# Writing the tokens' scales to DRAM as ten rows of 512 bytes, after a transpose on TensorE

## The chip, the core and the metric

The kernel runs on one core of one Trainium2 chip. The metric is the device time of one execution, in microseconds (us). Engines are named as in the profile: PE is TensorE (PEld its weight loads), DVE is VectorE, ACT is ScalarE, POOL is GpSimd, and SP is the engine that issues most of the transfers.

## What is computed

One encoder layer over 1280 tokens (1024 of a prompt, 256 of a sample) of width 1024, in float32. Only the beginning matters here:

```python
def _rms_norm(x, g, eps):
    xf = x.astype(jnp.float32)
    y = xf * lax.rsqrt(jnp.mean(xf * xf, axis=-1, keepdims=True) + eps)
    return (y * g.astype(jnp.float32)).astype(x.dtype)
...
    n = _rms_norm(h, g_mix, NORM_EPS)
    z = jnp.einsum('bsd,dc->bsc', n, w_in).astype(f32)
    cuts = np.cumsum([A_Q_COLS, A_K_COLS, A_V_COLS, B_Q_COLS, B_K_COLS]).tolist()
    qa, ka, va, qb, kb, vb = jnp.split(z, cuts, axis=-1)
```

Two attention mixers (A: four differential heads; B: eight query heads on two key heads), an output projection, an MLP of width 4096, a gated embedding and a last norm follow. All of that is the same before and after.

## The kernel before

The projection multiplies the tokens, scaled by `g_mix` but not yet by the norm, with blocks of `w_in`; the norm's factor, one number per token, is applied to the result. Each float32 operand is split into a high and a low part, and three matmuls are done for each product: high by high, high by low, low by high.

The factors are in `rstd1`, a tile of 128 partitions by 10 columns: token `128 t + p` stands at partition `p`, column `t`. Where tokens lie on partitions (units for B's q and k, and for v: `b_unit`, `va_unit`), a column of `rstd1` is used directly. Where tokens lie along the free dimension (`qk_unit`, for A's q and k), the factors are needed as a row that is the same on all 128 partitions: the tile `R`, 128 x 1280. It is made through DRAM: `rstd1` is written into the DRAM tensor `rd` in the order of tokens (L439), and `rd` is read back into `R`, broadcast to all partitions (L440). Since neighbouring elements of a row of `rstd1` are 128 tokens apart in `rd`, the write is made of 1280 single elements of 4 bytes.

The stages around it, in the order of the program:

- `b_unit(2, w_kv)`, woven with `va_unit(0, w_va0)`: B's k and v, and half of A's v, for the token tiles 0 to 9. Each token tile gives a PSUM tile `psb` (L241), which `norm_rope` turns into `ro` with many small operations on VectorE, ScalarE and POOL; TensorE transposes `ro` into `trb` two tiles later (L324).
- small constants (`gple`, `gmlp`, `gsub`, `lam_t`), then `rd` and `R`
- `b_unit(0, ...)` woven with `va_unit(1, ...)`, and then `b_unit(1, ...)` woven with `qk_a(0)`, the first that reads `R`.

Weights come in blocks. `load_w` brings 256 KB into `rawp` (a unit of 256 columns has four such blocks) or `rawa` (128 columns, two blocks), makes the high part on ScalarE (`whp` or `wha`, L176) and the low part on VectorE or POOL (`wlp` or `wla`, L177). Six buffers hold `rawp`, ten each hold `whp` and `wlp`. In what follows the twelve `rawp` of the units after the constants are counted from 1; number 6 is the second block of `va_unit(1)`.

Which instruction stands where in an engine's row is set by a scheduler that follows the program and a simulated time line; each engine then executes its row in order. Transfers issued by `dma` and `load` all stand in SP's row; loads of weights keep their order among themselves. `pp1` holds PSUM tiles, of which those of the tag "pb" (`psb`) have two buffers, used in turn.

Of the kernel before, what the change touches and what calls it, by code (L numbers as in the profile page):

```python
# [14 lines left out]
F32 = mybir.dt.float32  # L15
F32R = mybir.dt.float32r
F16 = mybir.dt.float16
AF = mybir.ActivationFunctionType
# [5 lines left out]
P = 128  # L24
# [5 lines left out]
NT = T // P  # L30
# [15 lines left out]
def encoder_kernel(ctx: ExitStack, tc: tile.TileContext, x, xT, pT, w_in, w_out, w_ff1, w_ff2, w_gate, w_proj,  # L46
# [39 lines left out]
    V, S, G, PE = nc.vector, nc.scalar, nc.gpsimd, nc.tensor  # L86
    dma = nc.sync.dma_start
# [9 lines left out]
    def pool(name, bufs=1, side=None, space=None, stack=None):  # L97
        kw = dict(name=name, bufs=bufs, reuse_waits="tile")
        if side:
            kw["side"] = side  # L100
        if space:
            kw["space"] = space
        return (stack or ctx).enter_context(tc.tile_pool(**kw))
# [14 lines left out]
    ident = cp.tile([P, P], F32, name="ident")  # L118
# [33 lines left out]
    rstd1 = cp.tile([P, NT], F32, name="rstd1")  # L152
# [55 lines left out]
    bp = pool("bp", side="left", bufs=2, stack=bs)  # L208
    ppj = pool("ppj", bufs=2, space=PSUM)
    pp1 = pool("pp1", bufs=1, space=PSUM, stack=bs)  # L210
# [224 lines left out]
    V.tensor_scalar(neglam, neglam, -LAM_INIT, None, op0=ALU.add)  # L435


    rd = dp.tile([1, T], F32, name="rd")
    dma(rd.rearrange("a (t p) -> p (a t)", p=P), rstd1)  # L439
    dma(R, rd.to_broadcast([P, T]))  # L440

    weave(b_unit(0, wload(1536, dma=load)), va_unit(1, wload(1280, dma=load)), 1.0)
# [1110 lines left out]
```

## Time and profile before

| what | value |
|---|---|
| median of 3 runs | 1733.48 us (1733.33 to 1734.53) |
| the profiled execution, time | 1731.98 us |
| the profiled execution, span from first to last instruction | 1730.2 us |
| PE busy | 1676.3 us (97% of the span) |
| DVE, ACT, POOL busy | 1180.3 us, 859.7 us, 703.0 us |
| mean granted clock of TensorE | 0.992 |
| DMA packets | 189111, of which 14512 under 512 B |

Times within the profile are counted from the start of the span. A row of a timeline gives start, length, engine, line, operation, output and inputs; what stands in brackets is how long the engine had been idle before it, and who released it. A row of the chain of waits gives start, length and what the time went to. A row of transfers gives their number, the KB of each, and the time from issue to landing.

### The profile page before, as it was taken

To read this page: it belongs to the slowest core of one execution; us is meant where nothing else is said; L and a number is where in the kernel's file an instruction comes from. 1 tells how busy PE (TensorE), PEld (TensorE's weight loads), DVE (VectorE), ACT (ScalarE), POOL (GpSimd) and SP (SyncE) were. 2 spreads that over 40 slices of the span, in tenths; PEclk is the share of its full clock that TensorE was granted. 3 is DMA by queue.
4 is the path that set the end of the run, shared out by engine and by line. 5 is a ranking of instruction groups with operands and counts; after the bars stand their busy time and mean duration, and the time that the engine had idled before them with its cause. 6 is when DMAs were issued, how large, how long until landed. Compare 5 with 4: busy or idle time off the path is not lost.

```text
span 1730.2 us, 27230 instructions
## 1 busy us (share of the span) xinstructions
PE 1676.3 (97%) x9848; PEld 1493.9 (86%) x9848; DVE 1180.3 (68%) x2104; ACT 859.7 (50%) x1730; POOL 703.0 (41%) x677
## 2 busy tenths in 40 slices
PE   8799999999899999998999999999999999999997
PEld 8799888888788888877999999998888888888886
DVE  7567578777877878578766666665764855354666
ACT  8423377776776757665323332333433333344554
POOL 1123455545564445346765656530533400001442
PEclk9999999999999999998999999999999999999999
DMA  9832573433963523382433433349676365532111
GB/s 320 218 117 100 179 189 113 128 110 93 257 187 120 157 76 108 103 257 97 140 138 130 154 124 137 128 167 388 205 233 194 123 208 190 174 113 83 39 43 49
DMA packets 189111, 263.60 MB, mean 152 GB/s; under 512 B 14512, under 2 KB 121904, under 8 KB 188976
## 3 DMA queue, kind: packets, MB, share of 16 engines
q1 hardware_dynamic: 187232, 256.60, 46.6%
q0 software_dynamic: 1600, 5.24, 1.0%
q8 instruction: 78, 1.28, 0.3%
q14 instruction: 57, 0.47, 0.1%
q10 hardware_dynamic: 144, 0.00, 0.0%
HBM read 175.29 MB, written 81.27 MB: 148 GB/s over the span
## 4 chain that ended last, share of the span: by engine, by line
PE 85%; DVE 5%; issue 3%; DMA 3%; ACT 2%; POOL 1%; SPq 0%; POOLq 0%; DVEq 0%; ACTq 0%
PE psa L241 6%; PE sc L569 6%; PE av L647 5%; PE psg L157 5%; PE pso L241 5%; PE psb L241 4%; PE tr L623 4%; PE psv L241 3%; PE psp L157 1%; DMA rawp<-in_w_in 1%; DMA h_sb<-in_w_out 1%; DVE pl L634 1%; DVE p L604 1%; PE f__16266 L157 1%; PE f__15226 L157 1%
## 5 line engine op out<-in xcount | busy, mean ns | idle before, releaser
L569 PE MATMUL sc<-kt,qt 128*128 128x512 f32 (+1 forms) x576 | 156.4, 390 | 11.3 <-ACT p L594 5.2
L1262 ACT ACTIVATE ao<-ar 128x1280 fp32r<-128x1280 f32 x56 | 71.3, 1274 | 191.1 <-PE f__16270 L157 37.9
L1264 DVE TENSOR_TENSOR ao<-ar,ao 128x1280 fp32r<-128x1280 f32 x56 | 95.4, 1705 | 98.0 <-ACT ao L1262 98.0
L634 DVE TENSOR_TENSOR pl<-tr,ph 128x512 fp32r<-128x512 f32 x204 | 137.9, 684 | 35.4 <-ACT ph L629 34.4
L629 ACT ACTIVATE ph<-tr 128x512 fp32r<-128x512 f32 x204 | 120.1, 595 | 58.2 <-PE tr L623 47.1
L241 PE MATMUL pso<-ow,mt 128*128 128x512 f32 x480 | 124.1, 402 | 4.1 <-DMA mt<-md 2.5
L569 PEld LDWEIGHTS sc<-kt,qt 128*128 128x128 f32 x576 | 98.4, 189 | 29.9 <-DVE mm L582 7.0
L1044 POOL TENSOR_SCALAR w1r<-w1r,gmlp 128x256 f32<-128x256 f32 x128 | 108.4, 863 | 38.5 <-DMA w1r<-in_w_ff 19.0
L623 PE MATMUL tr<-ident,p 128*128 128x128 f32 x768 | 115.7, 273 | 4.1 <-DVE pl L634 3.3
L157 PE MATMUL psg<-gw,n 128*128 128x512 f32 (+1 forms) x504 | 115.2, 384 | 0.0
L623 PEld LDWEIGHTS tr<-ident,p 128*128 128x128 f32 x768 | 91.6, 140 | 21.1 <-DVE pl L634 7.1
L157 PEld LDWEIGHTS psg<-gw,n 128*128 128x128 f32 x504 | 90.8, 188 | 19.5
L241 PEld LDWEIGHTS pso<-ow,mt 128*128 128x128 f32 x480 | 87.9, 191 | 21.7 <-DMA mt<-md 2.9
L647 PE MATMUL av<-ph,vt 128*128 128x256 f32 x544 | 103.0, 291 | 1.2 <-DVE o L695 0.5
L1052 ACT ACTIVATE w<-w1s 128x512 fp32r<-128x512 f32 x64 | 40.1, 628 | 125.3 <-POOL w1s L1070 6.8
L608 POOL TENSOR_SCALAR p<-p,rl 128x1024 f32<-128x1024 f32 x64 | 76.2, 1192 | 50.8 <-DVE rl L606 49.8
L586 DVE TENSOR_REDUCE mm<-sc 128x1 f32<-128x1024 f32 (+1 forms) x80 | 84.0, 1055 | 10.6 <-PE sc L569 10.0
L647 PE MATMUL av<-pl,vt 128*128 128x256 f32 x408 | 90.4, 303 | 0.2 <-DVE pl L634 0.2
L647 PEld LDWEIGHTS av<-ph,vt 128*128 128x128 f32 x544 | 82.8, 191 | 6.7 <-DVE osq L674 0.8
L594 ACT ACTIVATE p<-sc,mm 128x1024 f32<-128x1024 f32 x64 | 71.3, 1115 | 24.7 <-DVE mm L586 12.0
L1437 POOL TENSOR_TENSOR p_l<-pr,p_h 128x256 fp32r<-128x256 f32 x10 | 7.8, 782 | 182.7 <-ACT p_h L1436 182.7
L582 DVE CUSTOM_DVE_ANT_0 p<-sc,dist 128x1024 f32<-128x1024 f32 x64 | 77.5, 1217 | 5.7 <-PE tr L623 2.6
(1506 smaller groups left out, 4793.7 us busy)
## 6 DMA issues: line engine op xcount, KB each, us to landing
ar<-ad SPq DMA_DIRECT2D x56, 640.0 KB, 4.1
w2r<-in_w_ff SPq DMA_DIRECT2D x56, 512.0 KB, 4.4
qt<-qd SPq DMA_DIRECT2D x160, 128.0 KB, 3.0
ad<-q SPq DMA_DIRECT2D x64, 320.0 KB, 2.3
w1r<-in_w_ff SPq DMA_DIRECT2D x32, 512.0 KB, 3.8
ad<-qs SPq DMA_DIRECT2D x48, 320.0 KB, 2.2
md<-ml SPq DMA_DIRECT2D x40, 256.0 KB, 2.5
mt<-md SPq DMA_DIRECT2D x20, 512.0 KB, 4.8
```

The costliest lines, as they stand in the source:

```text
L157: PE.matmul(ps, a, b, start=start and i == 0, stop=stop and i == n - 1)
L241: PE.matmul(ps, a, b, start=i == 0, stop=i == n - 1)
L569: PE.matmul(ps[:, h0:h0 + n], shared["q"][:, cc, v, i * P:(i + 1) * P], kt[:, s0 + h0:s0 + h0 + n], start=v == 0, stop=v == 1)
L582: V.tensor_tensor_reduce(out=p[:, :sn], in0=ps[:, :sn], in1=dst_t[:, off:off + sn], scale=SLOPES[idx], scalar=3.0e38, op0=ALU.add, op1=ALU ...
L586: V.tensor_reduce(out=st["m", i][:, 0:1], in_=ps[:, :sn], axis=AX.X, op=ALU.max, negate=True)
L608: G.tensor_scalar(p[:, :sn], p[:, :sn], rl[:, 0:1], 1.0, op0=ALU.mult, op1=ALU.mult)
L623: PE.transpose(t[:, jj, i * P:(i + 1) * P], st["ws"][i][:, j * P:(j + 1) * P], ident)
L629: S.activation(ph, st["tr", j2], AF.Copy)
L634: V.tensor_tensor(pl, st["tr", j2], f(st["ph", j2][:]), op=ALU.subtract)
L647: PE.matmul(st["av"][:, :256], x_, y_, start=j2 == 0 and n == 0, stop=j2 == nj - 1 and n == len(pr) - 1)
L1044: G.tensor_scalar(r, r, gmlp[:, k:k + 1], 1.0, op0=ALU.mult, op1=ALU.mult)
L1264: V.tensor_tensor(ao[:, 1], a, f(ao[:, 0]), op=ALU.subtract)
```

## The change

`rstd1` is transposed on TensorE with the identity matrix into a PSUM tile of the tag "pb" (10 partitions by 128), copied to SBUF by ScalarE as `rr_t`, and written to `rd` from there: ten rows, each of 128 neighbouring tokens, 512 bytes. The read into `R` is the same.

```diff
+    rp = pp1.tile([P, 512], F32, tag="pb", name="rp", bufs=2)
+    PE.transpose(rp[:NT, :P], rstd1, ident)
+    rr_t = bp.tile([NT, P], F32, name="rr_t", bufs=1)
+    S.activation(rr_t, rp[:NT, :P], AF.Copy)
     rd = dp.tile([1, T], F32, name="rd")
-    dma(rd.rearrange("a (t p) -> p (a t)", p=P), rstd1)
+    dma(rd.rearrange("a (t p) -> (a t) p", p=P), rr_t)
     dma(R, rd.to_broadcast([P, T]))
```

Lines behind the change have numbers higher by 4: `rd`'s transfer is L439 before and L443 after, `R`'s L440 and L444.

SP's row, before, from the transfer `rd` on (`rawp` are weight blocks, here numbers 6 to 9; `vad` and `vbd` are stores of v):

```order
L439 DMA rd<-rstd_95 128x10x1
L94 DMA rawp<-in_w_in 128x2x256
L371 DMA vad_73<-vl 128x256
L371 DMA vad_74<-vl 128x256
L94 DMA rawp<-in_w_in 128x2x256 x2
L440 DMA R<-rd 128x1280
L94 DMA rawp<-in_w_in 128x2x256
```

The same place after:

```order
L94 DMA rawp<-in_w_in 128x2x256 x2
L371 DMA vad_73<-vl 128x256
L371 DMA vad_74<-vl 128x256
L94 DMA rawp<-in_w_in 128x2x256 x2
L352 DMA vbd_77<-vbl 128x128
L352 DMA vbd_78<-vbl 128x128
```

`rd` and `R` are gone from here, block 6 has moved into `rd`'s place, and 7 ahead of two stores. Both transfers now stand further on in SP's row, after the blocks of the next unit and the first `rawa`:

```order
L443 DMA rd<-rr_t 10x128
L319 DMA kd_72<-qkl 128x2x512
L94 DMA rawa<-in_w_in 128x4x128
L444 DMA R<-rd 128x1280
L94 DMA rawa<-in_w_in 128x4x128
L319 DMA kd_72<-qkl 128x2x256
```

TensorE's row at the border between the units, before (`trb` are transposes of `ro`, for tiles 7 and 8; `psb` is the first token tile of `b_unit(0)`):

```order
L241 MATMUL psv<-whp,xl 128x256
L324 MATMUL trb<-ident,ro 128x128
L241 MATMUL psb<-whp,xh 128x256
L324 MATMUL trb<-ident,ro 128x128
L241 MATMUL psb<-wlp,xh 128x256
```

And after:

```order
L241 MATMUL psv<-whp,xl 128x256
L324 MATMUL trb<-ident,ro 128x128
L439 MATMUL rp<-ident,rstd_95 10x128
L324 MATMUL trb<-ident,ro 128x128
L241 MATMUL psb<-whp,xh 128x256
```

The new transpose `rp` stands between the two others, and the first `psb` matmul behind them.

ScalarE's row a little later, before:

```order
L176 ACTIVATE whp<-rawp 128x512
L316 ACTIVATE qkl<-trb 128x512
L176 ACTIVATE wha<-rawa 128x512 x2
L284 ACTIVATE sq<-psb,rstd_95 128x256
L368 ACTIVATE vl<-psv,rstd_95 128x2x128
```

And after:

```order
L176 ACTIVATE whp<-rawp 128x512
L316 ACTIVATE qkl<-trb 128x512
L176 ACTIVATE wha<-rawa 128x512
L441 ACTIVATE rr_t<-rp 10x128
L176 ACTIVATE wha<-rawa 128x512
L284 ACTIVATE sq<-psb,rstd_95 128x256
```

The copy `rr_t` stands between the first two splits `wha` of A's weights. Further on, the rows of all engines are the same before and after but for a few neighbours that change places.

## Prediction

> **What bounds the kernel now.** I read the page first, then TensorE's waits, then the chain of waits around the change, and last the queue of SP, on which the changed transfer stands.
>
> ```profile
> PE 1676.3 (97%) x9848; PEld 1493.9 (86%) x9848; DVE 1180.3 (68%) x2104; ACT 859.7 (50%) x1730; POOL 703.0 (41%) x677
> ```
>
> TensorE is busy 97% of the span, so a change to a side transfer can only matter where TensorE stands still. The list of its waits, longest first (total, times, longest, in us), begins with the first of these rows:
>
> ```profile
> PE trb L324 <- DVE ro L302: 9.2, 2, 7.9
> ...
> PE pso L241 <- DMA mt<-md: 2.5, 1, 2.5
> ```
>
> One wait of 7.9 us is the longest of the whole kernel; the longest on a load later on, for `mt`, is 2.5. In the timeline of TensorE (start, us, engine, line) it stands here, at the border between the first projection units and the next ones:
>
> ```profile
> 65.96 0.27 PE L324 MATMUL trb<-ident,ro 128*128 128x128 f32 x1
> 65.99 0.36 PE L241 MATMUL psb<-whp,xh 128*128 128x256 f32 x1
> 74.29 0.47 PE L324 MATMUL trb<-ident,ro 128*128 128x128 f32 x1 [7.94 <-DVE ro L302]
> 74.42 0.56 PE L241 MATMUL psb<-wlp,xh 128*128 128x256 f32 x1
> ...
> 78.17 0.28 PE L241 MATMUL psv<-whp,xh 128*128 128x256 f32 x1
> 78.29 0.28 PE L241 MATMUL psv<-wlp,xh 128*128 128x256 f32 x1
> ...
> 81.83 0.28 PE L241 MATMUL psb<-whp,xh 128*128 128x256 f32 x1
> ```
>
> VectorE's `ro` is only the last link. The chain of waits tells what held it:
>
> ```profile
> 53.69 6.03 DMA rawp<-in_w_in
> ...
> 59.74 11.77 DMA rawp<-in_w_in
> ...
> 71.53 0.64 ACT whp L176
> ...
> 72.19 0.07 DVE wlp L177
> ...
> 73.31 0.25 DVE vbl L349
> ...
> 73.94 0.30 DVE ro L302
> ...
> 74.29 0.47 PE trb L324
> ```
>
> A block of weights (`rawp`, 256 KB) issued at 59.74 needed 11.77 us. ScalarE executes in order, so it sat on that block's split (`whp`) with the small operations of token tile 8 behind it; VectorE sat on `wlp` in the same way, and TensorE on the transpose of that tile. SP's queue shows what was sent just ahead of the slow block, and the rows of transfers (KB, us to landing) what it cost:
>
> ```profile
> 59.13 0.37 SPq L439 DMA_DIRECT2D rd<-rstd  x1
> 59.74 0.63 SPq L94 DMA_DIRECT2D rawp<-in_w_in  x1
> 60.47 0.89 SPq L371 DMA_DIRECT2D vad<-vl  x2
> 61.40 4.71 SPq L94 DMA_DIRECT2D rawp<-in_w_in  x2
> 71.37 0.34 SPq L440 DMA_DIRECT2D R<-rd  x1
> 71.80 0.39 SPq L94 DMA_DIRECT2D rawp<-in_w_in  x1
> ...
> 73.81 1.41 SPq L94 DMA_DIRECT2D rawp<-in_w_in  x3
> 75.27 0.46 SPq L94 DMA_DIRECT2D rawa<-in_w_in  x1
> ```
>
> ```profile
> gsub<-in_g_subln SPq DMA_DIRECT2D x1, 0.5 KB, 2.1
> vbd<-vbl SPq DMA_DIRECT2D x1, 64.0 KB, 9.4
> rd<-rstd SPq DMA_DIRECT2D x1, 5.0 KB, 12.2
> rawp<-in_w_in SPq DMA_DIRECT2D x1, 256.0 KB, 12.9
> rawp<-in_w_in SPq DMA_DIRECT2D x1, 256.0 KB, 4.8
> rawa<-in_w_in SPq DMA_DIRECT2D x1, 256.0 KB, 3.8
> ```
>
> The 5 KB of `rd` take 12.2 us, and everything in flight with it is slow: the `vbd` issued just before it takes 9.4, the `rawp` issued at 61.40 takes 12.9, while the same 256 KB take 4.8 when issued at 73.81 and 3.8 (the `rawa` after the one of 75.27) once the queue is quieter. So the single elements of `rd` clog the queue, the weights behind them come late, and TensorE stands on them. `gsub` has 128 single elements and lands in 2.1 us; `rd` has 1280 and takes 12.2. If both spread over 16 engines, 72 more elements each cost 10.1 us: an estimate of 0.14 us per element and engine.
>
> By the Trainium skill's page "DMA: Bandwidth & Descriptors" (section "Anatomy of one DMA — SWDGE (gpsimd) path") a transfer takes about 2.0 us plus its bytes over 436 GB/s, by which `rd` would be about 2 us before and after alike and the change worth nothing here; 12.2 us says that this fit does not hold for single elements on SP's queue, so I follow the row.
>
> **The change, step by step.** *The slow transfer leaves the spot.* The order puts `rawp` 6 and 7 where `rd` and `rawp` 6 stood. So `rawp` 6 goes out at 59.13, not 59.74. Its landing is what I must bound: 3.8 us (the quiet `rawa`) to 6.03 (the last of a burst of five, first row of the chain). Only small stores are under way at 59.13, but `rawp` 7 follows at once, so I take the row at 73.81, 4.8, which also had companions. Then `whp` starts at 59.13 + 4.8 + 0.02 = 63.95. From `whp` to the transpose the chain above takes 74.29 − 71.53 = 2.76 us, all in-order work on ScalarE and VectorE that stays, so the transpose can run at 66.71. TensorE is ready for it at about 66.1 (65.96 and two short transposes). The wait becomes 0.6 us in place of 7.94: a gain of 7.3, between 6.1 (landing 6.03, wait 1.8) and 7.9 (3.8, no wait).
>
> *The clock.* The stretches show TensorE's granted clock (third column from the end):
>
> ```profile
> 71.50:74.00 2.50, 0.00 (x0) 0.00 (x0) 1.70 (x8) 1.54 (x5) 0.45 (x1) 0.50 0.91 144
> 74.00:80.00 6.00, 5.71 (x34) 5.71 (x35) 4.08 (x12) 3.37 (x6) 0.00 (x0) 0.66 1.02 351
> 475.00:480.00 5.00, 3.33 (x16) 3.03 (x17) 1.49 (x5) 4.86 (x10) 3.67 (x4) 0.75 1.09 343
> ```
>
> ```profile
> 57.31 0.33 PE L324 MATMUL trb<-ident,ro 128*128 128x128 f32 x1 [1.22 <-DVE ro L302]
> ...
> 475.94 0.48 PE L569 MATMUL sc<-kt,qt 128*128 128x256 f32 x2 [2.21 <-DVE mm L586]
> ```
>
> The clock is halved during the wait and stays so until 78.17: the 17 matmuls from 74.42 to there take 3.75 us, against 17 x 0.117 = 2.0 at the later pace (78.17 to 78.29). That is 1.8 us more, and it goes if the wait is too short to halve the clock. The wait of 2.21 us near 476 was followed by a mean of 0.75 over 5 us, worth 1.25; after the 1.22 us wait at 57.31 matmuls ran at the full pace. With 0.6 us left I expect no dip: gain 1.8, bounds 0 and 1.8. The Trainium skill's page "TensorE: Matmul & The Clock Gate" (section "Part 1: The HAM clock gate") gives an idle window of about 3.4 us for the drop; by it a remaining wait under 3.4 us would cost no clock, by the row at 476 one of 2.2 already may, and the measurement decides.
>
> *What is added on TensorE.* One transpose of 128x10 between two others. The pair at 65.96 and 65.99 shows a transpose hardly moving the next matmul, the cold one at 74.29 lasts 0.47. I take 0.1, bounds 0 and 0.47. Its input, the last scale, is made in the stage before, and its PSUM buffer is that of token tile 8, whose readers stand ahead of `whp` 6. The first matmul of the next unit moves on to the buffer of tile 9, whose last reader is `vbl` (73.31 in the chain), ahead of `ro`, so it waits for nothing that the transpose doesn't wait for.
>
> *What is added on ScalarE, and whom it can hold.* The copy `rr_t` reads PSUM, as `vbl` does, with fewer columns filled:
>
> ```profile
> 49.59 0.37 ACT L348 ACTIVATE vbl<-psb,rstd 128x128 fp32r<-128x128 f32 x1
> ...
> 80.82 0.63 ACT L176 ACTIVATE wha<-rawa 128x512 fp32r<-128x512 f32 x1 [1.09 <-DMA rawa<-in_w_in]
> ```
>
> I take 0.3 us. It stands behind the first `wha`, which waits for the first `rawa`, and the second token tile of the next unit needs the PSUM buffer that `rr_t` reads. That tile's first matmul starts at 81.83, 7.5 us after the transpose, or 5.8 without the slow clock: 66.7 + 5.8 = 72.5 in the changed kernel. `rawa` before went out 3.9 us after SP came free of its wait for `rd` (71.37 to 75.27). Without that wait the block issued at 71.80 follows the one of 61.40 at about 62, so `rawa` goes out near 66 and, with the 5.5 us that it took before (75.27 to 80.82), lands at 71.5; `wha` 0.6 and `rr_t` 0.3 make 72.4. That just fits, 0.1 us ahead. It is the one tight place that the change adds. With a landing of 3.8 the margin is 1.8; a `rawa` sent 2 us later costs 1.9. I take a loss of 0.4 for this and for the next transpose (tile 9), whose `ro` follows block 9's `wlp`; bounds 0 and 1.9.
>
> *The moved transfers.* `rd` (ten rows) now goes out near 73 and `R` waits for it, with a `rawa`, stores of k and v, a `rawq` and a load of `kt` behind on SP. Nearest row for a tiny transfer: 2.1 us (`gsub`), upper end 12.2. None of those is needed soon, and `R` itself is first read at 146.6:
>
> ```profile
> L383 DVE SCALAR_TENSOR_TENSOR zl<-psa,R x6: 413/680/682, 146.6 to 193.2; 128x512 f32<-128x512 f32 x4, 128x256 f32<-128x256 f32 x2
> ```
>
> So `R` has some 65 us of cover and I cost it at nothing; without that cover it would be 2.1 plus its own 5.3 us landing. The order of all later work is the same but for two or three swapped neighbours, and nothing there runs by an absolute time, so I let the shift pass to the end.
>
> **Sum.** 7.3 + 1.8 − 0.1 − 0.4 = 8.6 us. The profiled execution took 1731.98 us (span 1730.2), so 1723.4 for it; it lies 1.5 below the median of the runs, 1733.48, against which I forecast 1724.9. About 0.2%, 3.5 us, is what a measurement of this kernel can tell from no change.
>
> **Rivals.** *The weights stay late for other reasons.* For it: a `vbd` store sent before `rd` was slow too, with 9.4 us. Against it: that store was still under way when `rd` began, and the `rawp` of 53.69, with four others ahead of it, took 6.03. If `rawp` 6 takes 7.5 us, `whp` starts at 66.65, the wait is 3.3, and the clock dips again for the 1.25 of the row at 476: gain 7.94 − 3.3 + 1.8 − 1.25 − 0.5 = 4.7, or 1728.8. Chance 0.15.
>
> *Bytes set the price, and the transfer was hidden.* Then the wait of 7.9 us has another cause, and the added transpose and copy leave the time as it is: 1733.5. The rows of 12.2 us (`rd`) and 12.9 us (`rawp`) stand against it. Chance 0.04. The Trainium skill's fit named above would have it so.
>
> *The gain is given back later*, because attention loads or the clock in later stages take it: TensorE waits 2.5 us for `mt` there. For a shifted but equal order I see no reason; half would be 1729.2. Chance 0.06.
>
> *Slower: `rr_t` holds a PSUM buffer.* If SP sends `rawa` no earlier than before, it lands at 80.8, `rr_t` ends at 81.7, and TensorE waits 9.2 us at the second tile, more than is won; with the clock dip the result is 1733.48 + 2 = 1735.5. It decides from a landing at about 80; at 72 it costs almost nothing. Against it: the wait for `rd` that held SP until 71.37 is gone. With what could lie beyond it, chance 0.03.
>
> **The numbers.** My forecast has the remaining 0.72, between 1722.8 (all bounds best, gain 9.7, and 1 us for the spread of the runs) and 1727.2 (6.1 + 1.8 − 0.1 − 1.5). The range for 8 in 10 takes in the first rival: 1722.8 to 1729.3. Faster by over 0.2% needs a time under 1730.0: the forecast, the first rival and part of the third, 0.90; within 0.2% the rest of those and the hidden transfer, 0.07; slower 0.03.
>
> **What would show it.** In the changed profile: `rd` landing in 2 to 3 us; the `rawp` issued near 59.1 landing within 6; TensorE's wait at the transpose under 2 us; a granted clock of 1.00 between 66 and 80; and some 1280 fewer packets under 512 B:
>
> ```profile
> DMA packets 189111, 263.60 MB, mean 152 GB/s; under 512 B 14512, under 2 KB 121904, under 8 KB 188976
> ```
>
> I am wrong if `rawp` 6 still takes over 7 us, or if a new wait of a `psb` matmul on `rr_t` of more than 2 us appears near 72.

## The result and the profile after

The changed kernel took 1722.73 us (median of five runs, 1719.94 to 1727.12), the kernel before, on the same chip, 1734.03 (five runs, 1733.33 to 1734.69). The ratio is 0.9938, with an interval of [0.9922, 0.9954]: about 11 us less. The profiled execution of the changed kernel is the longest of its five, 1727.12 us with a span of 1725.3.

The page's line of busy times hardly differs from that of before, one matmul and one ACT instruction more:

```profile
PE 1676.9 (97%) x9849; PEld 1492.5 (87%) x9849; DVE 1181.1 (68%) x2104; ACT 861.0 (50%) x1731; POOL 703.1 (41%) x677
```

TensorE's waits (total, times, longest) no longer hold one of 7.9 us; the line of the transposes has one wait of 1.9:

```profile
PE sc L573 <- ACT p L598: 6.0, 7, 2.1
...
PE trb L324 <- DVE ro L302: 1.9, 1, 1.9
```

The chain of waits of the changed kernel, at the place where that of before ran through a weight block of 11.77 us, now runs along TensorE itself:

```profile
57.70 0.30 DVE ro L302
...
58.05 0.33 PE trb L324
58.38 4.35 PE psb L241 x24
62.73 5.61 PE psv L241 x48
68.35 0.11 PE trb L324
68.45 0.11 PE rp L439
68.56 0.11 PE trb L324
68.67 0.71 PE psb L241 x6
```

The three transposes at 68.35 to 68.67 are those of token tile 7, of the scales, and of tile 8; the last of them had the 7.94 us wait before. SP's queue and the rows of transfers (KB, us to landing; the `rawp` is that of 59.57 with block 6) show why:

```profile
59.57 1.18 SPq L94 DMA_DIRECT2D rawp<-in_w_in  x2
60.85 0.89 SPq L371 DMA_DIRECT2D vad<-vl  x2
61.83 1.01 SPq L94 DMA_DIRECT2D rawp<-in_w_in  x2
...
65.47 0.46 SPq L94 DMA_DIRECT2D rawa<-in_w_in  x1
...
72.13 0.36 SPq L443 DMA_DIRECT2D rd<-rr_t  x1
...
74.00 0.47 SPq L444 DMA_DIRECT2D R<-rd  x1
```

```profile
rawp<-in_w_in SPq DMA_DIRECT2D x1, 256.0 KB, 2.8
...
R<-rd SPq DMA_DIRECT2D x1, 640.0 KB, 5.1
```

Block 6 lands in 2.8 us where it took 11.77. On ScalarE its split (63.04) and the copy of the scales come with time to spare: `rr_t` ends at 72.1, and the first matmul that needs its PSUM buffer is in the chain at 74.40.

```profile
63.04 0.62 ACT L176 ACTIVATE whp<-rawp 128x512 fp32r<-128x512 f32 x1
...
71.32 0.63 ACT L176 ACTIVATE wha<-rawa 128x512 fp32r<-128x512 f32 x1 [0.86 <-DMA rawa<-in_w_in]
71.86 0.25 ACT L441 ACTIVATE rr_t<-rp 10x128 f32<-10x128 f32 x1
```

One thing is worse here. The stretches of the changed kernel (granted clock third from the end) show a slow piece soon behind the wait of 1.89 us that ends at 58.05 (the clock is halved from 59.17 on), and none at the old place:

```profile
58.00:66.00 8.00, 7.95 (x55) 7.95 (x56) 7.78 (x28) 5.42 (x17) 3.09 (x4) 0.79 0.91 272
66.00:72.00 6.00, 6.00 (x54) 5.98 (x53) 4.85 (x13) 4.32 (x10) 0.00 (x0) 1.00 0.96 300
```

That wait was 1.22 in the profile of before; VectorE waits there for the load of `lam_t` with `ro` behind it. Instruction by instruction, TensorE runs 5.9 us earlier than before at the transpose of tile 8 (68.40 against 74.29), some 7.6 where the old halved clock ended (7.65 between 130 and 200 us), and 4.85 at the end of the program (1731.98 against 1727.12 us).

### The profile page after: what moved, and what is told of

Same layout as the page of the kernel before. It is cut to its first block, busy times and chain, and to the rows that moved or that the text cites. A ratio compares the mean times of both kernels' runs of the same rounds, so it can differ in the third digit from the quotient of the medians.

```text
span 1725.3 us, 27233 instructions
## 1 busy us (share of the span) xinstructions
PE 1676.9 (97%) x9849; PEld 1492.5 (87%) x9849; DVE 1181.1 (68%) x2104; ACT 861.0 (50%) x1731; POOL 703.1 (41%) x677
## 4 chain that ended last, share of the span: by engine, by line
PE 78%; DMA 8%; DVE 7%; issue 3%; ACT 2%; POOL 1%; SPq 0%; DVEq 0%; ACTq 0%; POOLq 0%
PE psg L157 6%; PE sc L573 6%; PE av L651 5%; PE psa L241 4%; PE pso L241 4%; PE tr L627 4%; PE psb L241 3%; PE psv L241 2%; PE psp L157 2%; DMA w2r<-in_w_ff 1%; DVE wo L1269 1%; DVE p L586 1%; DVE pl L638 1%; DMA xt<-in_x 1%; DVE p L608 1%
## 5 line engine op out<-in xcount | busy, mean ns | idle before, releaser
L573 PE MATMUL sc<-kt,qt 128*128 128x512 f32 (+1 forms) x576 | 156.8, 391 | 12.2 <-ACT p L598 6.0
```

Of the source, the lines that this page charges most:

```text
L573: PE.matmul(ps[:, h0:h0 + n], shared["q"][:, cc, v, i * P:(i + 1) * P], kt[:, s0 + h0:s0 + h0 + n], start=v == 0, stop=v == 1)
```

## Experiments: what the single elements did

Two readings of the profile of before had to be told apart. The first: the 1280 single elements clog the transfers around them. The second: SP stands at `R`, waiting for `rd`, and so sends the blocks behind late. Later runs ask what it is about single elements that costs.

**dummy1280: the changed kernel plus the old write, idle.** Nobody reads `rx`, so nothing on SP waits for it.

```diff
+    rx = dp.tile([1, T], F32, name="rx")
+    dma(rx.rearrange("a (t p) -> p (a t)", p=P), rstd1)
     rp = pp1.tile([P, 512], F32, tag="pb", name="rp", bufs=2)
```

> The changed kernel, with the write of 1280 single elements put back at its old place into a tensor that nobody reads; rd in ten rows and R stay where the change has them. Theory 1 (the single elements clog the queue, and weight block 6 behind them comes late): the idle write takes about 12 us, block 6 about 12 us, TensorE waits 7 to 8 us at the transpose near 66 us, and the time goes back to 1733, within 2. Theory 2 (what counted was SP itself, held by R's wait for rd until 71 us): nothing waits for the idle write, so the time stays with the changed kernel, 1723, within 2.

Measured: 1734.16 us, ratio to before 1.0002 [0.9993, 1.0011]. All of the gain is gone, and TensorE's wait is back at the same transpose, longer than the 7 to 8 us expected:

```profile
75.57 0.48 PE L324 MATMUL trb<-ident,ro 128*128 128x128 f32 x1 [9.40 <-DVE ro L302]
```

The clog alone does it; the second reading falls.

**rows_old_place: the kernel before, with ten rows at the old place.** The rows come from a VectorE product, without the transpose and the copy, so the values in `R` are not the tokens' scales.

```diff
-    dma(rd.rearrange("a (t p) -> p (a t)", p=P), rstd1)
+    rr_t = bp.tile([NT, P], F32, name="rr_t", bufs=1)
+    V.tensor_scalar(rr_t, mean_m[:NT, :], rstd1[:NT, 9:10], None, op0=ALU.mult)
+    dma(rd.rearrange("a (t p) -> (a t) p", p=P), rr_t)
```

> The kernel before, with rd written as ten rows of 512 bytes at the old place, and R's wait right behind it as before. The rows come from a small VectorE product (constants times a scale), so that there is no transpose on TensorE and no copy on ScalarE; the scales in R are not the right ones. Theory 1 (single elements clog): rd lands in 2 to 4 us, block 6 in 3 to 6, the wait at the transpose is under 1 us, and the time is that of the changed kernel, 1723, within 3. Theory 3 (the place in SP's row and R's wait cost, not the form): 1733, within 2.

Measured: 1724.67 us, 0.9942 [0.9929, 0.9954], the whole gain without moving the write. What is left of TensorE's waits at the transposes is the one near 58 and one of 1 us for tile 9:

```profile
58.82 0.33 PE L324 MATMUL trb<-ident,ro 128*128 128x128 f32 x1 [2.17 <-DVE ro L302]
71.43 0.33 PE L324 MATMUL trb<-ident,ro 128*128 128x128 f32 x1 [1.05 <-DVE ro L302]
```

**elem_late: the kernel before, its single elements some 40 us later**, behind a store of `vad`.

```diff
+    marks = {}
...
-                dma(vad[2 * u + j][t * P:(t + 1) * P], f(hl[:, j]))
+                marks[u, t] = dma(vad[2 * u + j][t * P:(t + 1) * P], f(hl[:, j]))
...
+    weave(b_unit(0, wload(1536, dma=load)), va_unit(1, wload(1280, dma=load)), 1.0)
     rd = dp.tile([1, T], F32, name="rd")
-    dma(rd.rearrange("a (t p) -> p (a t)", p=P), rstd1)
+    with tc.issue_after(marks[1, 4].ins):
+        dma(rd.rearrange("a (t p) -> p (a t)", p=P), rstd1)
     dma(R, rd.to_broadcast([P, T]))
-
-    weave(b_unit(0, wload(1536, dma=load)), va_unit(1, wload(1280, dma=load)), 1.0)
```

> The kernel before with its 1280 single elements, but sent some 40 us later, behind a store of v of the fifth token tile of the next unit; R follows it. No transpose and no copy are added. Theory 1 (they clog whatever is in flight, and only the weights near 60 us hurt): the write takes about 12 us near 100 us, stores beside it are slow too, TensorE does not wait for it, and the time is 1722, within 3, as with rows. Rival (single elements cost wherever they stand): 1728 or more.

Measured: 1721.79 us, 0.9932 [0.9919, 0.9944]. SP's queue shows the same slow write, up to 9.1 us until `R` could be sent (about 12 expected), at a place where nothing that TensorE needs is under way:

```profile
99.63 0.67 SPq L444 DMA_DIRECT2D rd<-rstd  x1
108.68 0.32 SPq L445 DMA_DIRECT2D R<-rd  x1
```

So there are two cures, form and place, and each is worth the whole gain. They do not add up: the changed kernel, which has both, gains no more (0.9938).

**elem_act: the kernel before, the elements on ScalarE's queue.**

```diff
-    dma(rd.rearrange("a (t p) -> p (a t)", p=P), rstd1)
+    S.dma_start(rd.rearrange("a (t p) -> p (a t)", p=P), rstd1)
```

> The kernel before, its 1280 single elements sent from ScalarE's queue in place of SP's; R still waits for them on SP. Theory 1 with the engines as what is shared (single elements take the time of the DMA engines, whichever queue they come from): weight blocks still land late, in 5 to 13 us, and the wait at the transpose is 3 to 8 us: 1727 to 1734. Rival (it is the order within SP's own queue): the blocks land in 3 to 6 us, R's wait on SP holds a few blocks, and the time is 1723 to 1726.

Measured: 1730.63 us, 0.9974 [0.9961, 0.9987]. TensorE still waits 5.84 us in place of 7.94: another issuing engine does not part the elements from SP's transfers. The elements left 1.6 us earlier here (57.51 against 59.13 us) and `R`, which needs them, was sent as much earlier (69.81 against 71.37), so most of the 2.1 us may be the earlier start and not the other queue. In this round of runs (elem_act, dummy2560, dummy384, lam_late) the kernel before took 1736.1 us, some 2 us more than in the others, and that makes these four ratios look a little better.

```profile
72.94 0.47 PE L324 MATMUL trb<-ident,ro 128*128 128x128 f32 x1 [5.84 <-DVE ro L302]
```

## Experiments: what sets the price of single elements

**dummy2560 and dummy384: twice the write, and three columns of it**, idle, in the changed kernel, at the old place.

```diff
+    for i in range(2):
+        rx = dp.tile([1, T], F32, name=f"rx{i}")
+        dma(rx.rearrange("a (t p) -> p (a t)", p=P), rstd1)
```

```diff
+    rx = dp.tile([1, T], F32, name="rx")
+    dma(rx.rearrange("a (t p) -> p (a t)", p=P)[:, 7:], rstd1[:, 7:])
```

> The changed kernel with two idle writes of 1280 single elements each at the old place. By a price per element the second adds its 10 to 12 us: the wait at the transpose is 18 to 21 us, the clock stays halved to some 4 us behind it, and the time is 1743 to 1746. If the two overlap on the engines (the price is one of latency, not of work): 1733 to 1736.

> The changed kernel with an idle write of 384 single elements (three columns of the scales) at the old place, which nobody reads. Theory 1 with a price per element: 0.14 us per element and engine, 24 elements per engine, 3.4 us on top of the landing of block 6 (2.8 us in the changed kernel), so it lands near 65.5 and the wait at the transpose is 2 to 3 us, with or without a halved clock behind it: 1724 to 1727. Rival (any write of single elements costs the whole 8 us, by a state into which it puts the queue): 1733.

Measured: 1745.03 us, 1.0048 [1.0032, 1.0064], and 1733.21 us, 0.9983 [0.9972, 0.9993]. The waits, first with 2560 elements, then with 384:

```profile
85.97 0.47 PE L324 MATMUL trb<-ident,ro 128*128 128x128 f32 x1 [19.65 <-DVE ro L302]
```

```profile
75.37 0.48 PE L324 MATMUL trb<-ident,ro 128*128 128x128 f32 x1 [8.80 <-DVE ro L302]
```

A second write adds 10 us, as expected, but 384 elements wait nearly as long as 1280 (9.40). A price for each element does not give that. The expectation of dummy384 (a wait of 2 to 3 us) was missed, and with it the estimate of 0.14 us per element and engine.

**dummy128, dummy_far, dummy_pad, dummy_line: fewer elements, or the same number farther apart in DRAM.** All are idle writes in the changed kernel at the old place: one column; all 1280, each in 512 bytes of its own; all 1280, 8 bytes apart; all 1280, 64 bytes apart.

```diff
+    rx = dp.tile([1, T], F32, name="rx")                                   # dummy128
+    dma(rx.rearrange("a (t p) -> p (a t)", p=P)[:, 9:], rstd1[:, 9:])
```

```diff
+    rx = dp.tile([T, P], F32, name="rx")                                   # dummy_far
+    dma(rx.rearrange("(t p) c -> p t c", p=P)[:, :, 0], rstd1)
```

```diff
+    rx = dp.tile([P, 2 * NT], F32, name="rx")                              # dummy_pad
+    dma(rx.rearrange("p (t c) -> p t c", c=2)[:, :, 0], rstd1)
```

```diff
+    rx = dp.tile([T, 16], F32, name="rx")                                  # dummy_line
+    dma(rx.rearrange("(t p) c -> p t c", p=P)[:, :, 0], rstd1)
```

> The changed kernel plus an idle write of one column of the scales (128 single elements, neighbours in DRAM) at the place of the old write. Measured so far at that place: 1280 elements give a wait of 9.4 us at the transpose and a ratio of 1.000 to before, 384 elements 8.8 us and 0.998, two writes of 1280 19.7 us and 1.005. Theory N (price by the number of elements, already hurt by 384): 0.14 us x 8 per engine = 1.1 us, so a wait of 0 to 2.5 us and a ratio of 0.994. Theory W (a price for each write of single elements, whatever their number) and theory L (elements that lie in the same 512-byte row of DRAM wait on each other: 128 of them in each row, and the rows run side by side, so that 1, 3 or 10 rows take the same time): a wait of 8 to 9.5 us and a ratio of 0.998 to 1.000.

> The changed kernel plus an idle write of all 1280 single elements, each into a row of 512 bytes of its own in DRAM; source, count and place in the queue are those of the 1280 packed elements, which gave a wait of 9.4 us at the transpose. Theory L (elements in one row of DRAM wait on each other): nothing to wait on, a wait of 0 to 3 us and a ratio of 0.994. Theories W (a price for each such write) and N (by number): 8.5 to 10 us again and a ratio of 1.000.

> The changed kernel plus an idle write of all 1280 single elements in the other order: the ten of a partition lie next to each other in DRAM, 8 bytes apart, so that they stay single elements. In a row of 512 bytes lie 64 elements of 6 or 7 partitions, in place of 128 of 128 partitions. Theory L: half the elements in a row, a wait of 3 to 6 us, ratio 0.996 to 0.998. Theories W and N: 8.5 to 10 us and 1.000.

> The changed kernel plus an idle write of all 1280 single elements, each 64 bytes from the next in DRAM: eight elements in a stretch of 512 bytes. So far: 4 bytes apart 9.4 us of wait at the transpose, 8 bytes apart 7.7 us, 512 bytes apart none; 128 elements 4 bytes apart 7.2 us. If elements disturb each other only within 64 bytes or less: a wait of 0 to 2.5 us and a ratio of 0.994. If they do so within 512 bytes, or within a larger piece of DRAM: a wait of 4 to 9 us and a ratio of 0.996 to 1.000.

Measured, with the earlier ones beside them:

| idle write | apart in DRAM | wait at the transpose, us | ratio to before |
|---|---|---|---|
| 1280 elements | 4 bytes | 9.40 | 1.0002 [0.9993, 1.0011] |
| 384 elements | 4 bytes | 8.80 | 0.9983 [0.9972, 0.9993] |
| 128 elements | 4 bytes | 7.20 | 0.9983 [0.9973, 0.9993] |
| 1280 elements | 8 bytes | 7.68 | 0.9993 [0.9983, 1.0002] |
| 1280 elements | 64 bytes | 0.75 | 0.9934 [0.9915, 0.9953] |
| 1280 elements | 512 bytes | none | 0.9942 [0.9927, 0.9957] |

In TensorE's timeline the transpose of tile 8, for 128 elements, for 64 bytes, and for 512 bytes:

```profile
75.17 0.48 PE L324 MATMUL trb<-ident,ro 128*128 128x128 f32 x1 [7.20 <-DVE ro L302]
```

```profile
66.86 0.33 PE L324 MATMUL trb<-ident,ro 128*128 128x128 f32 x1 [0.75 <-DVE ro L302]
```

```profile
66.04 0.33 PE L324 MATMUL trb<-ident,ro 128*128 128x128 f32 x1
```

In the last of them the next transpose, tile 9's, waits 0.98 us; rows_old_place had 1.05 there.

And the transfers themselves: 1280 single elements land in 4.8 us when 64 bytes apart, and in 4.5 when 512 apart (this row and block 6's, from the latter), against 12.2 for `rd` before. Block 6 behind them lands in 4.1; behind 128 packed elements, in the chain of waits, it needs 10.71:

```profile
rx<-rstd SPq DMA_DIRECT2D x1, 5.0 KB, 4.8
```

```profile
rx<-rstd SPq DMA_DIRECT2D x1, 5.0 KB, 4.5
...
rawp<-in_w_in SPq DMA_DIRECT2D x1, 256.0 KB, 4.1
```

```profile
61.69 10.71 DMA rawp<-in_w_in
```

So what sets the price of one such write is not that its elements are single, and hardly how many they are. It is where in DRAM they lie: 4 and 8 bytes apart they make TensorE wait 7 to 9 us, 64 bytes apart 0.75 us, which does not show in the time. The price per element (theory N) falls with the third row, the price per write (theory W) with the last two. Theory L is right in kind, but its size of 512 bytes is wrong, since eight elements share 512 bytes in the fifth row, and so is its halving for 8 bytes apart: 7.68 against the expected 3 to 6.

The packets of the transfers show when the stall comes; the elements are those under 512 B. First the kernel before, from 60 to 62 us and in the 8 us behind; then the elements 64 bytes apart, from 59.5 to 61.5 and in the 8 us behind:

```profile
DMA packets 1476, 0.11 MB, mean 54 GB/s; under 512 B 1318, under 2 KB 1476, under 8 KB 1476
DMA packets 553, 0.54 MB, mean 67 GB/s; under 512 B 41, under 2 KB 552, under 8 KB 552
```

```profile
DMA packets 1531, 0.16 MB, mean 79 GB/s; under 512 B 1320, under 2 KB 1531, under 8 KB 1531
DMA packets 2997, 2.47 MB, mean 309 GB/s; under 512 B 195, under 2 KB 2996, under 8 KB 2996
```

Both times the packets of the elements are through in 2 us, and the price is paid behind them: 67 GB/s in place of 309. What holds the later packets the profile does not show. That writes to one small piece of memory wait on each other is one reading that fits the six rows. Not parted from it is another, the size of the whole piece that is written: the four writes that pay lie within 0.5 to 10 KB, the two that do not are spread over 80 and 640 KB. (Ten rows of 512 bytes in 5 KB, as in rows_old_place, pay nothing, so a small piece alone is not enough.) Where between 8 and 64 bytes the price begins, and why 128 elements stall nearly as long as 1280, stays open. The Trainium skill's page "DMA: Bandwidth & Descriptors" (section "Specifications") says that below 512 bytes an engine reads, modifies and writes; all six rows are below that, and only four of them pay, so that rule alone does not give the price.

## Experiments: the size of the gain and its spread

**changed_again: the changed kernel once more.**

> The changed kernel once more, for a second trace. Its runs spread over 7 us, those of before over 1.4. If the spread is the clock, which fell for a while near 59 us in the first trace: 1722.7, within 4, and the trace shows other times at which the clock is halved, with a time that goes with their sum at 0.5 us per us. If it is not: the same halvings and another time.

Measured: 1723.99 us (1720.61 to 1725.95), 0.9941 [0.9928, 0.9953]. Its profiled execution took 1720.61 us, and the border between the units shows what differs from the first one:

```profile
57.07 0.33 PE L324 MATMUL trb<-ident,ro 128*128 128x128 f32 x1 [1.50 <-DVE ro L302]
...
65.94 0.27 PE L324 MATMUL trb<-ident,ro 128*128 128x128 f32 x1
```

```profile
66.00:80.00 14.00, 14.00 (x122) 14.00 (x121) 9.26 (x24) 6.57 (x16) 5.81 (x6) 1.00 0.97 293
```

With 1.50 us of wait near 57 the clock was not halved; with 1.89 it was. Here tile 8's transpose runs at 65.94 against 74.29 before, 8.35 us earlier, and the end of the old slow clock adds 1.8: 10.1 us gained at this place, as ScalarE's instructions from 166 to 400 us confirm (10.1 to 10.2). The records show the halved clock in pieces of 3.4 us or whole multiples (but for the last, which the end of the program cuts), each worth some 1.7 us of matmuls.

The length of a wait alone does not decide whether such a piece follows: waits of 1.97 us (elem_late, ending at 59.29), 2.17 (rows_old_place, 58.82) and 2.37 (dummy_pad, 58.50) were followed by none. In the clock records of each of the 14 traces the halved pieces start whole multiples of 3.413 us apart, on a grid that lies elsewhere in each execution: in changed_again at 445.71, 746.08, 769.98 and 800.70, that is 88, 7 and 9 steps. In the first profile the whole wait of 1.89 us fell between two marks of its grid (55.76 and 59.17), and the halved piece began at the second mark; of the 2.37 us in dummy_pad 1.81 fell before a mark (57.94) and the rest behind it. Between 10 and 1700 us of the 14 traces, each step at full clock in which TensorE stood for more than 1.81 us in all was followed by a halved one, none was in which it stood for less than 1.38, and between these both occur.

Laid instruction by instruction beside each other, the first profile's execution falls behind this one by 2.5 us at the border (the longer wait and its slow piece), 1.1 more near 230 us, 1.9 near 470, and 1.0 near 1260: together the 6.5 us between 1727.12 and 1720.61. The largest of the later ones begins with a wait on VectorE that has no counterpart here (rows of the first profile):

```profile
469.65 0.77 PE L573 MATMUL sc<-kt,qt 128*128 128x256 f32 x2 [2.27 <-DVE mm L590]
```

A second halved piece lies there. The kernel before had the same wait (2.21, near 476), so it is no product of the change. Which of these waits come, and which of them cost a slow piece, differs from one execution to the next; that makes the 6.5 us between these two. So the expectation was met in part: the halved pieces lie elsewhere, but their sum alone does not give the difference.

**lam_late: the changed kernel with `lam_t`'s load and its small operations behind the next two units.** The block of L427 to L435 moves unchanged below the `weave` of `b_unit(0)`:

```diff
-    load(lam_t.rearrange("p a b -> p (a b)"), lams.to_broadcast([P, 256]))
...
     weave(b_unit(0, wload(1536, dma=load)), va_unit(1, wload(1280, dma=load)), 1.0)
...
+    load(lam_t.rearrange("p a b -> p (a b)"), lams.to_broadcast([P, 256]))
```

> The changed kernel with the load of the lambda vectors and its small operations (lam_t to neglam) written after the next units, so that the order moves them behind the first weight blocks. In the changed kernel VectorE waits 3 us for lam_t near 54, and TensorE 1.5 to 1.9 us at a transpose near 57, behind which one trace shows a halved clock. If that is the next wait in line: the wait near 57 falls under 0.7 us and the time is 1721.5, within 1.5, 1 to 3 less than the changed kernel. If another wait takes its place (the first weight block, which ScalarE awaits at the same time): as the changed kernel, 1723.5, within 1.

Measured: 1720.91 us (1720.15 to 1726.88), 0.9912 [0.9898, 0.9926]. The wait near 57 is gone, and the median is the lowest of the study. That it is faster than the changed kernel is not shown: its interval overlaps that of the first run of the changed kernel (0.9898 to 0.9926 against 0.9922 to 0.9954; the second has 0.9928 to 0.9953), and the kernel before was some 2 us slower in this round than in theirs. Its profiled execution, the longest of its five, has a new wait at the next border, with one halved piece behind it:

```profile
67.33 0.55 PE L241 MATMUL psb<-whp,xh 128*128 128x256 f32 x1 [2.31 <-DVE vbl L349]
```

## Why the prediction came out as it did

The direction and the mechanism were right. The median of 1722.73 lies 2.2 us below the forecast and 0.07 us below the lower end of the range, 1722.8, for which every bound had been taken at its best and 1 us allowed for the spread: the forecast was too cautious.

- *What bounds.* That the elements of `rd` hold up block 6 and with it TensorE is shown by dummy1280 (the wait comes back with the elements alone) and rows_old_place (it goes with the form alone).
- *The wait.* Predicted 0.6 us left of 7.94, measured none. The mis-sized term is block 6's landing: 4.8 us taken, 2.8 measured (issued at 59.57, not 59.13), so `whp` ran at 63.04, not 63.95. Its lower bound, 3.8, was not low enough either. The step behind it was taken too short: from `whp` to the end of `ro` it is 3.3 us here (63.04 to 66.33) and 3.4 in changed_again (61.88 to 65.29), where 2.76 to the transpose was read from a profile in which everything else had long been waiting. The two errors partly cancel, which was luck.
- *The clock.* The 1.8 us at the old place came as predicted: 1.00 between 66 and 80 us in changed_again. Not foreseen was that the wait one tile earlier, 1.22 us before, could grow to 1.89 and bring a halved piece of its own. The prediction let the shift pass to the end because nothing later ran by an absolute time; the grid of the clock does, so an equal order, shifted, can meet other halved pieces. The price of a dip in the first rival, 1.25, was read from a stretch that ends at 480, inside the piece (477.50 to 480.91); a whole piece costs 1.7. The Trainium skill's page "TensorE: Matmul & The Clock Gate" (section "Part 1: The HAM clock gate") speaks of an idle window of about 3.4 us; the pieces here are of that length, but 1.89 us of wait was enough to start one.
- *The added waits.* Predicted loss 0.4, measured none. `rawa` went out at 65.47 (66 predicted) and `rr_t` ended at 72.1 (72.4 predicted), but the matmul behind it came at 74.24 in the timeline (74.40 in the chain), not 72.5, since the longer wait and the slow piece at 59 had held TensorE: a margin of 2.1 us in place of 0.1. In changed_again, without that piece, everything is earlier and 1.5 us are left:

```profile
70.00 0.25 ACT L441 ACTIVATE rr_t<-rp 10x128 f32<-10x128 f32 x1
```

```profile
71.78 0.28 PE L241 MATMUL psb<-whp,xh 128*128 128x256 f32 x1
```

- *The moved transfers.* As predicted: `R` was sent 1.87 us after `rd`, for which it had to wait, and landed in 5.1 us. The packets under 512 bytes fell by 1286 (1280 predicted):

```profile
DMA packets 187835, 263.60 MB, mean 153 GB/s; under 512 B 13226, under 2 KB 120628, under 8 KB 187700
```

- *The sum.* With the measured terms it is 7.94 + 1.8 − 0.1 = 9.6 us in place of 8.6; the place itself shows 10.1 in changed_again, the medians 11.3. The rest is smaller than the spread told of above, and no run explains it.
- *The estimate per element* is the step that failed. It set `gsub`, a load of 128 single elements into SBUF in 2.1 us, beside `rd`, a store into DRAM, and put the difference down to their number. A store of 128 elements (dummy128) stalls nearly as long as one of 1280. The sum did not rest on it, since the row of 12.2 us carried the argument; the forecast for 384 elements went wrong by 6 us (2 to 3 us of wait against 8.80). The profile of before could have told: its 1280 elements are through the engines in 2 us.

The rivals: weights late for other reasons and a new PSUM wait did not come; that bytes set the price is refuted by dummy_far and dummy_line, which move the same 5 KB as dummy1280, and by dummy128, which moves a tenth. The Trainium skill's fit that the prediction names beside this rival ("DMA: Bandwidth & Descriptors", section "Anatomy of one DMA — SWDGE (gpsimd) path") is given there for transfers of the gpsimd path, so its miss here says nothing of that path. Of the third, a part came true in the first profile alone: 2.8 of its 7.65 us were lost again later on, while changed_again kept all of its 10.1.

## What to carry to other kernels

A small store into DRAM whose single elements lie side by side can hold up everything that is under way for some 7 to 10 us, even with 128 of them, the fewest tried: look for a big load that is slow right behind it, and not only for the store's own wait. It is cured by writing rows or by sending it where no weights are awaited; each gave the same, and moving it to another queue did not. Elements 64 bytes apart did no harm either, but only as a write that nobody read: reading such a spaced tensor back was not tried. Price a store by a store: a load of the same shape told nothing of it.

## What the runs showed that I had not expected

The 128 packed elements, 512 bytes in all, cost TensorE 7.2 us, and 1280 elements at 64 bytes 0.75. The granted clock falls in whole pieces of 3.4 us on a grid of its own: a wait of 1.89 us that fell into one step of it brought a piece, one of 2.37 us that was split by a mark did not. One piece is 1.7 us, so that a gain of a few us shows only over several runs on each side.
